# A hybrid decoder layer on one core: output-projection weights cast one step ahead, other casts and loads of the last two blocks put elsewhere

## The chip, the cores and the metric

The kernel runs on one core of one Trainium2 chip. Its time is the device time of one execution in microseconds (us), as the median of several runs. Beside the times stands one profiled execution, from which all rows below are taken. The engines are PE (matrix multiplications), DVE (VectorE), ACT (ScalarE), POOL (GpSimd) and SP, which here only issues transfers (DMA). Each engine works through its own list of instructions strictly in order: an instruction that waits holds back all that stand behind it on that engine.

## The reference

One layer of a decoder, for a prompt of 2048 tokens and 32 sample tokens (8 sequences of 4), all in float32. Cut to what the change touches:

```
z = rmsnorm(x, n1) @ w_in                 # split into hq, hf, hi, hg, sq, sk, sv, ga, gb
o_hg = hgrn_recurrence(q, log f, 1 - f, v, s0)      # 4 heads, state 128 x 128
y_a = (rmsnorm(o_hg) * silu(hg)) @ w_up_a           # 512 -> 1024
o_b = sliding-window attention with sinks (8 query heads, 2 kv heads)
y_b = o_b @ w_up_b                                   # 512 -> 1024
m = sigmoid(ga) * y_a + sigmoid(gb) * y_b
x = x + m @ w_o                                      # output projection, 1024 x 1024
x = x + relu(rmsnorm(x, n2) @ w_ff1)**2 @ w_ff2      # 1024 -> 4096 -> 1024
```

Of the sample tokens, each sequence starts from a state of its own and returns the new one.

## The kernel before

Activations lie transposed: features on the 128 partitions, tokens along the row. The prompt is worked in four blocks of 512 tokens (block 0 to 3; the last also carries the 32 sample tokens, so its row is 544 long and is worked in two segments of 288 and 256). After the four blocks the feed-forward part runs for all tokens. In blocks 2 and 3 (`zs` in the code) the gates ga and gb have been computed beforehand, between blocks 1 and 2, and are only loaded. In a tile's name the digit behind the letters is the block (`l_uab26`: block 2, unit 6); the profile leaves buffer numbers out, so there it is `l_uab`.

**Split precision.** Every matrix product is done as three: a float32 operand is split into a high part (ACT rounds it, line L257, tiles `h_...`) and a low part (DVE subtracts the high part from the original, L258, tiles `l_...`), and PE adds high*high, high*low and low*high. A weight unit of 128x1024 numbers is loaded by SP (`r_...`), and is usable by PE when ACT's cast and DVE's subtraction of it are done. `unit` and `unit_rows` issue the load, the cast and the subtraction. The three tiles of a unit take three of 12 buffers in one pool, so a load also waits until an older unit's last reader is done.

**Order.** The program is written in one order, and a scheduler puts each engine's instructions into a fixed list, by its own view of when they are ready. `pin(...)` (`keep_in_program_order`) keeps an instruction where the program has it. At run time nothing is reordered.

**One block**, in the order of time:

1. The input projections (`hi`, `hf`, `hg`, `sq`, `skv`) and the attention of four chunks (`b2c`: block 2), interleaved.
2. The levels of the recurrence (`hgrn_levels`): for m = 1, 2, 4, ... 64 PE does many small products (`lv_b2g0_1`, L771), and DVE two multiplications (L776, L777) and one predicated copy (L788) for each of two groups of heads. A level needs DVE's results of the one before. The sample tokens have two short levels of their own (`lv_b3s`).
3. The recurrence over four chunks: state update on DVE (L1204), normalisation (`on`, L1164), transposition (L1174). In block 3 the four heads of the sample tokens follow: PE multiplies the value products `vb` (made by DVE, L1226) with the keys (`us`, L1233), and DVE adds them to each state `S`. Between them stand matrix products of `y_b`.
4. `y_b` (`ybb`): eight column tiles j, with units of `w_up_b` (`ubb`) for two tiles each.
5. `y_a` (`yab`), called gate a here: eight column tiles, units of `w_up_a` (`uab`) for two tiles each. For each tile DVE gates (`ga`, L1258), POOL (for the last tiles DVE) adds the other branch (L1298), and `m` is split by ACT (L257) and DVE (L258).
6. The output projection (`wob`), in four steps n = 0, 2, 4, 6 of two column tiles, with two units each (`l_wob240` and `l_wob241` are the units of step 4). In step 0 the contraction index k runs outside, so both tiles end together; in the other steps the tiles follow each other. DVE evicts each tile and adds the residual row held in `x1` (L1394), ACT squares it for the next norm (L241 the first, L244 the others), POOL writes it out.

Beside this, blocks 0 and 2 prepare sums for the feed-forward part: `fr_load` loads rows, and `fr_sums` does four DVE additions (L605 to L608) whose results POOL writes out. `fr_at` says after which column tile they are written.

Of the kernel before, what the change touches and what calls it, by code (L numbers as in the profile page):

```python
# [16 lines left out]
P = 128  # L17
# [26 lines left out]
def tile_hybrid_step(  # L44
# [186 lines left out]
    class Norm:  # L231
# [6 lines left out]
        def add(u, x, eng=nc.gpsimd):  # L238
            if u.acc is None:
                u.acc = carry[:, 0:u.n]  # L240
                nc.scalar.activation(u.acc, x, AF.Square)  # L241
# [390 lines left out]
    for bi in range(nblk):  # L632
# [276 lines left out]
        fr_at = {("b", 0): lambda: fr_load(0), ("b", 5): fr_sums, ("b", 6): lambda: fr_load(1), ("a", 3): fr_sums} if zs and not odd else {}  # L909
# [229 lines left out]
        if smp:  # L1139
            gens.append(hgrn_levels(qS, kS, fS, aS, LEVELS[:2], NS, NS, f"{B}s", sres, SV[:, 2048:2144] if bt > gc else SV[:, 1024:1120]))  # L1140
        rnd, hg_at = 0, (2, 3, 4, 6)
        while gens:
# [12 lines left out]
            rnd += 1  # L1155

# [28 lines left out]
        for c in range(ncb):  # L1185
# [19 lines left out]
            on = hgrn_out(ops, P, N)  # L1205
            if tail is not None:
                hgrn_tail(*tail)
            tail = (on, P, fW, c * P, N)
        if smp:
# [8 lines left out]
            for h in range(HH):  # L1218
# [7 lines left out]
                nc.vector.tensor_tensor(  # L1226
                    vb[0:NS].rearrange("p (b e) -> p b e", b=DB),
                    vS[:, h * P:(h + 1) * P].unsqueeze(1).broadcast_to([NS, DB, P]),
                    m_b[0:NS].unsqueeze(2).broadcast_to([NS, DB, P]), ALU.mult)
# [149 lines left out]
        rings = [hg_ps, tp_ps if last_b else hg_ps, sw_ps, mm_ps, hg_ps, sw_ps, mm_ps, hg_ps]  # L1379
        for n in range(0, KD, 2):  # L1380
# [369 lines left out]
```

## Time and profile before

| what | us |
| --- | --- |
| median of 3 runs | 2822.58 (2820.04 to 2824.71) |
| span of the profiled execution, first to last instruction | 2810.0 |
| PE busy in it | 2730.1 |
| DVE busy | 1791.2 |
| ACT busy | 1110.0 |
| POOL busy | 490.9 |

The runs' times take in what lies before the first and behind the last instruction, so the median stands 12.6 us above the span of the profiled execution. In its trace block 1's output projection ends at about 740 us; block 2 lies at 965 to 1206, block 3 at 1206 to 1501, and the feed-forward part fills the rest.

### The profile page before, as it was taken

Reading aid. Unit: us, or ns where it says so; the run is one execution under the profiler, and the core shown is the slowest. Engines: PE = TensorE matmul, PEld = TensorE weight load, DVE = VectorE, ACT = ScalarE, POOL = GpSimd, SP = SyncE. Lnnn points to the kernel's source line nnn. Section 1 sums busy time; section 2 is a strip of 40 time slices with the busy share of each in tenths; the row PEclk is TensorE's granted clock in tenths of the full one; section 3 lists DMA queues with packets and bytes.
Section 4 is the critical chain, followed back from the end, with each engine's and each line's share of the span. In section 5 each row is a group of like instructions: output and inputs, shape, how many; then the busy total and the mean of one; then the engine's idle time right before and its main releaser. Section 6 shows DMA issues by size and latency. Waiting matters only on the chain.

```text
span 2810.0 us, 50089 instructions
## 1 busy us (share of the span) xinstructions
PE 2730.1 (97%) x20053; PEld 2403.9 (86%) x20053; DVE 1791.2 (64%) x2905; ACT 1110.0 (40%) x2070; POOL 490.9 (17%) x782
## 2 busy tenths in 40 slices
PE   8999999999999999899999999999999999999998
PEld 7778888788899977677898888878888999999998
DVE  5675746746774385637667777765567777654556
ACT  4542445423344353335334333434344233343332
POOL 1100211002300102320231221220012343320001
PEclk9999999999999999999999999999999999999999
DMA  5237662377743424652365544796566444485553
GB/s 190 75 103 237 208 198 76 97 242 256 251 126 115 144 76 149 219 160 67 105 210 184 181 145 150 265 317 222 190 200 215 147 161 135 155 291 184 189 187 119
DMA packets 344481, 487.60 MB, mean 174 GB/s; under 512 B 23432, under 2 KB 220824, under 8 KB 344248
## 3 DMA queue, kind: packets, MB, share of 16 engines
q1 hardware_dynamic: 289112, 329.10, 37.5%
q0 software_dynamic: 42880, 140.22, 13.8%
q10 hardware_dynamic: 12256, 15.08, 1.5%
q8 instruction: 157, 2.57, 0.4%
q14 instruction: 76, 0.62, 0.1%
HBM read 353.64 MB, written 130.68 MB: 172 GB/s over the span
## 4 chain that ended last, share of the span: by engine, by line
PE 78%; DMA 6%; DVE 6%; issue 5%; ACT 2%; POOL 2%; SPq 0%; POOLq 0%; DVEq 0%; ACTq 0%
PE f L1581 6%; PE f L1582 6%; PE f L1580 6%; PE fB_f L264 4%; PE fB_f L266 3%; PE fB_f L265 3%; PE fD_f L264 2%; PE fD_f L266 2%; PE fD_f L265 2%; PE ps_hfb L684 2%; PE fB_z L264 1%; PE fB_z L266 1%; PE fB_z L265 1%; PE wob L1390 1%; PE gab L166 1%
## 5 line engine op out<-in xcount | busy, mean ns | idle before, releaser
L1582 PE MATMUL f<-f2S,lw2T 128*128 128x264 f32 (+1 forms) x576 | 184.4, 320 | 2.0 <-DVE lw2T L152 2.0
L1580 PE MATMUL f<-f2S,hw2T 128*128 128x264 f32 (+1 forms) x576 | 184.5, 320 | 1.6 <-ACT hw2T L151 1.6
L1581 PE MATMUL f<-f2S,hw2T 128*128 128x264 f32 (+1 forms) x576 | 184.0, 319 | 0.0
L264 PE MATMUL fB_f<-S,w1T_f 128*128 128x264 f32 (+1 forms) x384 | 123.2, 322 | 3.1 <-ACT c_f L327 2.2
L152 DVE TENSOR_TENSOR lw2T<-lw2T,hw2T 128x1024 fp32r<-128x1024 f32 x64 | 78.2, 1224 | 69.7 <-ACT hw2T L151 68.8
L265 PE MATMUL fB_f<-S,w1T_f 128*128 128x264 f32 (+1 forms) x384 | 122.5, 319 | 0.0
L1580 PE MATMUL f<-f2A,h_w2B 128*128 128x264 f32 (+1 forms) x384 | 122.4, 319 | 0.0
L1581 PE MATMUL f<-f2A,h_w2B 128*128 128x264 f32 (+1 forms) x384 | 122.3, 319 | 0.0
L1582 PE MATMUL f<-f2A,l_w2B 128*128 128x264 f32 (+1 forms) x384 | 122.3, 318 | 0.0
L266 PE MATMUL fB_f<-S,w1T_f 128*128 128x264 f32 (+1 forms) x384 | 122.0, 320 | 0.0
L151 ACT CAST hw2T<-lw2T 128x1024 fp32r<-128x1024 f32 x64 | 67.2, 1051 | 137.2 <-DMA lw2T<-w_T 137.2
L1582 PEld LDWEIGHTS f<-f2S,lw2T 128*128 128x128 f32 x576 | 108.4, 188 | 10.4 <-DVE lw2T L152 2.9
L1580 PEld LDWEIGHTS f<-f2S,hw2T 128*128 128x128 f32 x576 | 108.8, 189 | 9.9 <-ACT hw2T L151 2.4
L1388 PE MATMUL wob<-m_b,h_wob 128*128 128x512 f32 (+2 forms) x320 | 113.1, 353 | 3.2 <-ACT h_wob L257 3.2
L1390 PE MATMUL wob<-m_b,l_wob 128*128 128x512 f32 (+2 forms) x320 | 112.4, 353 | 3.0 <-DVE l_wob L258 2.8
L1581 PEld LDWEIGHTS f<-f2S,hw2T 128*128 128x128 f32 x576 | 108.8, 189 | 7.6
L1389 PE MATMUL wob<-m_b,h_wob 128*128 128x512 f32 (+2 forms) x320 | 112.5, 352 | 0.0
L152 DVE TENSOR_TENSOR f2S<-f2S 128x1024 fp32r<-128x1024 f32 (+1 forms) x64 | 78.9, 1240 | 41.3 <-ACT f2S L151 40.9
L257 ACT CAST w1T_f<-w1r_f 128x512 fp32r<-128x512 f32 x128 | 77.1, 619 | 69.7 <-DVE w1r_f L300 29.7
L258 DVE TENSOR_TENSOR w1T_f<-w1r_f,w1T_f 128x512 fp32r<-128x512 f32 x128 | 87.4, 688 | 26.0 <-ACT w1T_f L257 25.7
L1507 POOL DMA_DIRECT2D u_A<-c_f x106 | 57.4, 541 | 236.1 <-DVE c_f L1491 225.1
L1507 POOL DMA_DIRECT2D u_S<-s_f x144 | 77.7, 541 | 109.0 <-DVE s_f L1502 92.4
(845 smaller groups left out, 9256.8 us busy)
## 6 DMA issues: line engine op xcount, KB each, us to landing
w1r_f<-w_ff SPq DMA_DIRECT2D x64, 512.0 KB
lw2T<-w_T SPq DMA_DIRECT2D x64, 512.0 KB
rw2B<-w_ff SPq DMA_DIRECT2D x48, 512.0 KB
f2S<-u_S SPq DMA_DIRECT2D x32, 528.0 KB
ws<-w_ff SPq DMA_DIRECT2D x32, 512.0 KB
r_wob<-w_o SPq DMA_DIRECT2D x32, 512.0 KB
f2S<-u_S SPq DMA_DIRECT2D x32, 512.0 KB
u_S<-s_f POOLq DMA_DIRECT2D x96, 132.0 KB, 2.3
```

The source lines that it names most:

```text
L152: pin(nc.vector.tensor_tensor(lo, F(lo), F(hi), ALU.subtract), on)
L258: pin(nc.vector.tensor_tensor(dl, src, F(dh), ALU.subtract), on)
L264: nc.tensor.matmul(ps, wh, ah, start=(first and k == 0), stop=False, skip_group_check=not first)
L265: nc.tensor.matmul(ps, wh, al, start=False, stop=False, skip_group_check=not first)
L266: nc.tensor.matmul(ps, wl, ah, start=False, stop=(last and k == 3), skip_group_check=not first)
L1388: nc.tensor.matmul(p, wh, ah, start=(k == 0), stop=False)
L1389: nc.tensor.matmul(p, wh, al, start=False, stop=False)
L1390: nc.tensor.matmul(p, wl, ah, start=False, stop=(k == KD - 1))
L1507: nc.gpsimd.dma_start(us[o][u.n // 4][u.n % 4 * P:(u.n % 4 + 1) * P, u.t0:u.t0 + u.ln], y_)
L1580: nc.tensor.matmul(ps, wh, ah, start=first, stop=False, skip_group_check=cont)
L1581: nc.tensor.matmul(ps, wh, al, start=False, stop=False, skip_group_check=cont)
L1582: nc.tensor.matmul(ps, wl, ah, start=False, stop=lastk, skip_group_check=cont)
```

## The change

1. The second `fr_sums` of block 2 is written after column tile 6 of gate a instead of tile 3.
2. In blocks 2 and 3 the units of `w_up_b` are issued at other places: unit 0 before the levels, unit 2 behind them, units 4 and 6 in chunks 1 and 2 of the recurrence. Units 2, 4 and 6 are pinned there.
3. The sample tokens' value products `vb` are pinned: they stay behind the recurrence.
4. In blocks 2 and 3 the residual rows `x1` are loaded during gate a (at j = 2, 4, 6, 6). Each load is held by a one-column DVE copy from a cast weight tile into `x1`, so that it can't be issued sooner. The loads are on POOL's queue, as before.
5. In all blocks the units of a step of the output projection are loaded and cast one step ahead, before the evictions of the step in front of it; the first eviction and the first square of a step are pinned behind them.

The diff, cut to its core:

```
-            ("b", 6): lambda: fr_load(1), ("a", 3): fr_sums} ...
+            ("b", 6): lambda: fr_load(1), ("a", 6): fr_sums} ...
...
+        def ub_unit(j, on=False):
+            return unit([... w_ub ... j * P:j * P + 256 ...], 4, f"ub{B}{j}", on)
+        ubs = {0: ub_unit(0)} if zs else {}
         rnd, hg_at = 0, (2, 3, 4, 6)
         while gens:                            # the levels
...
+        if zs:
+            ubs[2] = ub_unit(2, True)
...
             on = hgrn_out(ops, P, N)           # chunk c of the recurrence
+            if zs and c in (1, 2):
+                ubs[2 * c + 2] = ub_unit(2 * c + 2, True)
...
-                nc.vector.tensor_tensor(vb ...)
+                pin(nc.vector.tensor_tensor(vb ...))
...
-                ub = unit(... w_ub ...)
+                ub = ubs[j] if zs else ub_unit(j)
...
+                if j == 2:
+                    x1 = x1_tile()
+                for k in {2: (0,), 4: (2,), 6: (4, 6)}.get(j, ()):
+                    x1_load(k, F(ua[1])[:, 0, 0:1])   # copy into x1[:, k, 0:1], then the load of rows k, k+1
...
+        uo_next = wo_units(0)
         for n in range(0, KD, 2):
-            uo = [unit_rows(w_o, 4 * kh, 4, n * P, 2 * P, ...) for kh in range(2)]
+            uo = uo_next
...
+            ahead = n + 2 < KD
+            if ahead:
+                uo_next = wo_units(n + 2)
             for j in range(2):
-                    nc.vector.scalar_tensor_tensor(xo, ps[j][i], 0.5, xo, ALU.mult, ALU.add)
-                n2.add(x1[:, n + j], nc.vector if last_b else nc.gpsimd)
+                    pin(nc.vector.scalar_tensor_tensor(xo, ps[j][i], 0.5, xo, ...), ahead and i == j == 0)
+                n2.add(x1[:, n + j], nc.vector if last_b else nc.gpsimd, ahead and j == 0)
```

In the built program the change moves instructions on every engine. Three places on DVE matter below. A row is a line of the program, an operation, the tile written and the tiles read, and its size; the line numbers of the changed kernel are some 10 to 30 higher.

First, DVE in the levels of block 2, around m = 8 and 16. Before:

```order
L788 COPY_PREDICATED SV_b2_9399<-cu_88,lv_b2g1_8_10354 128x16x8
L779 TENSOR_TENSOR SV_b2_9399<-SV_b2_9399 128x32 x2
L975 TENSOR_TENSOR sg_11957<-snk_136,cf_86 128x8
L1146 COPY pb_b2_10047<-SV_b2_9399 128x1 x2
L977 TENSOR_REDUCE srows_11959<-sg_11957 128x2
L258 TENSOR_TENSOR l_ubb26_11016<-r_ubb26_11012,h_ubb26_11015 128x1024
L776 TENSOR_TENSOR W0_b2_9397<-W0_b2_9397,SV_b2_9399 128x4x8x16
L720 SCALAR_TENSOR_TENSOR W1_b2_9398<-tg_b2_2_0_p_10422,W1_b2_9398 128x512
```

The same place in the changed kernel:

```order
L779 TENSOR_TENSOR SV_b2_9399<-SV_b2_9399 128x64
L788 COPY_PREDICATED SV_b2_9399<-cu_88,lv_b2g1_8_10361 128x16x8
L779 TENSOR_TENSOR SV_b2_9399<-SV_b2_9399 128x32 x2
L1152 COPY pb_b2_10047<-SV_b2_9399 128x1 x2
L776 TENSOR_TENSOR W0_b2_9397<-W0_b2_9397,SV_b2_9399 128x4x8x16
L720 SCALAR_TENSOR_TENSOR W1_b2_9398<-tg_b2_2_0_p_10429,W1_b2_9398 128x512
L777 TENSOR_TENSOR W0_b2_9397<-W0_b2_9397,SV_b2_9399 128x4x8x16
L788 COPY_PREDICATED SV_b2_9399<-cu_88,lv_b2g0_16_10433 128x8x16
```

The cast of unit 6 of `w_up_b` no longer stands in the levels. The same holds for units 2 and 4, which stood at m = 1 and just ahead of m = 8, and for the three of block 3; of block 3's levels the first `vb` is gone as well. At m = 1 the order of the rest moved too: DVE's first two multiplications of that level now stand behind the last split of the attention (`ob`), and 59 of PE's 64 small products of that level behind the attention's last product, where before the 32 of the first group stood ahead of it.

Second, DVE in gate a of block 2, where unit 6 of `w_up_a` is cast. Before:

```order
L258 TENSOR_TENSOR m0_b2_11063<-ga_b2_10883,m0_b2_11063 128x512
L605 TENSOR_TENSOR fr12_11035<-fr11_11034 128x512
L1258 SCALAR_TENSOR_TENSOR ga_b2_10883<-ga_b2_10883,yab24_0_11165 128x512
L606 TENSOR_TENSOR fr12_11035<-fr12_11035,fr10_11033 128x512
L607 TENSOR_TENSOR fr11_11034<-fr10_11033,fr11_11034 128x512
L608 TENSOR_TENSOR fr10_11033<-fr10_11033,fr12_11035 128x512
L258 TENSOR_TENSOR l_uab26_11162<-r_uab26_11159,h_uab26_11161 128x1024
L258 TENSOR_TENSOR m1_b2_11064<-ga_b2_10883,m1_b2_11064 128x512
```

In the changed kernel:

```order
L1269 SCALAR_TENSOR_TENSOR ga_b2_10911<-ga_b2_10911,yab23_0_11137 128x512
L258 TENSOR_TENSOR m0_b2_11063<-ga_b2_10911,m0_b2_11063 128x512
L1269 SCALAR_TENSOR_TENSOR ga_b2_10911<-ga_b2_10911,yab24_0_11162 128x512
L258 TENSOR_TENSOR l_uab26_11157<-r_uab26_11154,h_uab26_11156 128x1024
L1297 COPY x1_b2_11117<-l_uab26_11157 128x1
L258 TENSOR_TENSOR m1_b2_11064<-ga_b2_10911,m1_b2_11064 128x512
```

The four `fr` additions have left the place ahead of `l_uab26`. From tile 0 on the gating of a tile and the split of the same tile alternate, where before tiles 0 and 1 were both gated ahead of the first split.

Third, DVE from the end of gate a to step 4 of the output projection in block 2. Before:

```order
L1258 SCALAR_TENSOR_TENSOR ga_b2_10883<-ga_b2_10883,yab27_0_11216 128x512
L1298 TENSOR_TENSOR ga_b2_10883<-ga_b2_10883,pb_b2_10047 128x512
L258 TENSOR_TENSOR m1_b2_11064<-ga_b2_10883,m1_b2_11064 128x512
L258 TENSOR_TENSOR l_wob201_11249<-r_wob201_11246,h_wob201_11248 128x1024
L1394 SCALAR_TENSOR_TENSOR x1_b2_11233<-wob20_0_11252,x1_b2_11233 128x512
L1394 SCALAR_TENSOR_TENSOR x1_b2_11233<-wob21_0_11253,x1_b2_11233 128x512
L258 TENSOR_TENSOR l_wob220_11322<-r_wob220_11319,h_wob220_11321 128x1024
L258 TENSOR_TENSOR l_wob221_11328<-r_wob221_11325,h_wob221_11327 128x1024
L1394 SCALAR_TENSOR_TENSOR x1_b2_11233<-wob22_0_11331,x1_b2_11233 128x512
L605 TENSOR_TENSOR fr22_11307<-fr21_11306 128x512
L258 TENSOR_TENSOR l_wob240_11411<-r_wob240_11408,h_wob240_11410 128x1024
```

In the changed kernel, in two pieces, with nothing between them:

```order
L258 TENSOR_TENSOR m1_b2_11064<-ga_b2_10911,m1_b2_11064 128x512
L605 TENSOR_TENSOR fr12_11035<-fr11_11034 128x512
L1319 TENSOR_TENSOR ga_b2_10911<-ga_b2_10911,pb_b2_10047 128x512
L606 TENSOR_TENSOR fr12_11035<-fr12_11035,fr10_11033 128x512
L607 TENSOR_TENSOR fr11_11034<-fr10_11033,fr11_11034 128x512
L608 TENSOR_TENSOR fr10_11033<-fr10_11033,fr12_11035 128x512
L258 TENSOR_TENSOR m1_b2_11064<-ga_b2_10911,m1_b2_11064 128x512
```

```order
L258 TENSOR_TENSOR l_wob201_11253<-r_wob201_11250,h_wob201_11252 128x1024
L258 TENSOR_TENSOR l_wob220_11309<-r_wob220_11306,h_wob220_11308 128x1024
L1423 SCALAR_TENSOR_TENSOR x1_b2_11117<-wob21_0_11257,x1_b2_11117 128x512
L258 TENSOR_TENSOR l_wob221_11315<-r_wob221_11312,h_wob221_11314 128x1024
L1423 SCALAR_TENSOR_TENSOR x1_b2_11117<-wob20_0_11256,x1_b2_11117 128x512
L1423 SCALAR_TENSOR_TENSOR x1_b2_11117<-wob23_0_11336,x1_b2_11117 128x512
L258 TENSOR_TENSOR l_wob240_11388<-r_wob240_11385,h_wob240_11387 128x1024
L258 TENSOR_TENSOR l_wob241_11394<-r_wob241_11391,h_wob241_11393 128x1024
L1423 SCALAR_TENSOR_TENSOR x1_b2_11117<-wob22_0_11335,x1_b2_11117 128x512
```

The `fr` additions now stand between the gating of the last tile and `l_wob201`. The first unit of step 2 is cast ahead of both evictions of step 0. Of the evictions of step 2 the one of the second tile (`wob23`), which is not pinned, stands ahead of both casts of step 4, and the pinned one of the first tile (`wob22`) behind them. On SP the loads of the third and fourth pair of output-projection units still follow the loads for the third `fr` sums, which wait until the results of the second have been written.

More of the change, by code (lines that the diff above doesn't have):

```diff
@@ L907, in fr_sums @@
             ff_sums(0, None, r, k, True, q)
-        fr_at = {("b", 0): lambda: fr_load(0), ("b", 5): fr_sums, ("b", 6): lambda: fr_load(1), ("a", 3): fr_sums} if zs and not odd else {}
+        fr_at = {("b", 0): lambda: fr_load(0), ("b", 5): fr_sums, ("b", 6): lambda: fr_load(1), ("a", 6): fr_sums} if zs and not odd else {}
         if not zs:
@@ L1140, in tile_hybrid_step @@
             gens.append(hgrn_levels(qS, kS, fS, aS, LEVELS[:2], NS, NS, f"{B}s", sres, SV[:, 2048:2144] if bt > gc else SV[:, 1024:1120]))
+        def ub_unit(j, on=False):
+            return unit(
+                [(kv * HD, (kv + 1) * HD, w_ub[kv * 256:(kv + 1) * 256, j * P:j * P + 256].rearrange("(k p) c -> p k c", p=HD)) for kv in range(NKV)],
+                4, f"ub{B}{j}", on)
+        ubs = {0: ub_unit(0)} if zs else {}
         rnd, hg_at = 0, (2, 3, 4, 6)
@@ L1282, in tile_hybrid_step, with x1_tile, x1_load @@
         a_acts = [(oa[:, 0, k, :], oa[:, 1, k, :]) for k in range(4)]
+        def x1_tile():
+            return op(6, F32, "x1_" + B)[:, 0:KD * T].rearrange("p (k t) -> p k t", k=KD)
+        def x1_load(k, after=None):
+            if after is not None:
+                nc.vector.tensor_copy(x1[:, k, 0:1], after)
+            nc.gpsimd.dma_start(x1[:, k:k + 2], kmaj(xT, k, 2, off[sb] + z0, T))
         mT = [op(2 + g, F32R, f"m{g}_{B}")[:, 0:8 * T].rearrange("p (s k t) -> p s k t", s=2, k=4) for g in range(2)]
@@ L1312, in tile_hybrid_step @@
         c0 = z0
-        x1 = op(6, F32, "x1_" + B)[:, 0:KD * T].rearrange("p (k t) -> p k t", k=KD)
-        for k in range(0, KD, 2):
-            nc.gpsimd.dma_start(x1[:, k:k + 2], kmaj(xT, k, 2, off[sb] + z0, T))
+        if not zs:
+            x1 = x1_tile()
+            for k in range(0, KD, 2):
+                x1_load(k)
         todo = []
@@ L1379, in tile_hybrid_step, with wo_units @@
         rings = [hg_ps, tp_ps if last_b else hg_ps, sw_ps, mm_ps, hg_ps, sw_ps, mm_ps, hg_ps]
+        def wo_units(n):
+            return [unit_rows(w_o, 4 * kh, 4, n * P, 2 * P, f"wo{B}{n}{kh}") for kh in range(2)]
+        uo_next = wo_units(0)
         for n in range(0, KD, 2):
-            uo = [unit_rows(w_o, 4 * kh, 4, n * P, 2 * P, f"wo{B}{n}{kh}") for kh in range(2)]
+            uo = uo_next
             ps = [[rings[j](f"wo{B}{j}_{t0}")[:, 0:ln] for (t0, ln) in segs] for j in (n, n + 1)]
@@ L1393, in tile_hybrid_step @@
                     xo = x1[:, n + j, t0:t0 + ln]
[L1394 to L1395 removed]
+                    pin(nc.vector.scalar_tensor_tensor(xo, ps[j][i], 0.5, xo, ALU.mult, ALU.add), ahead and i == j == 0)
+                n2.add(x1[:, n + j], nc.vector if last_b else nc.gpsimd, ahead and j == 0)
                 nc.gpsimd.dma_start(x1d[sb][(n + j) * P:(n + j + 1) * P, z0:z0 + T], x1[:, n + j])
```

13 lines of the change are left out of this document (5 added, 8 removed).

## The prediction

> **What bounds the kernel.** I began with the page: the span, the busy times, and the chain that ended last.
>
> ```profile
> span 2810.0 us, 50089 instructions
> PE 2730.1 (97%) x20053; PEld 2403.9 (86%) x20053; DVE 1791.2 (64%) x2905; ACT 1110.0 (40%) x2070; POOL 490.9 (17%) x782
> PE 78%; DMA 6%; DVE 6%; issue 5%; ACT 2%; POOL 2%; SPq 0%; POOLq 0%; DVEq 0%; ACTq 0%
> ```
>
> PE is busy for 2730.1 of 2810.0 us. The change adds no product and takes none away, so all it can win is in the 80 us in which PE stands still, and in stretches where PE runs at a lower clock. I therefore asked for PE's waits in the two places that the change rewrites most: blocks 2 and 3 (first fence), and block 1's output projection (second). The columns are: who waits, for whom, total us, times, longest.
>
> ```profile
> PE lv_b2g L771 <- DVE SV_b L788: 4.4, 1, 4.4
> PE yab L167 <- DVE l_uab L258: 3.8, 1, 3.8
> PE wob L1388 <- ACT h_wob L257: 3.2, 2, 1.7
> PE lv_b3s L771 <- issue: 2.4, 1, 2.4
> PE lv_b3g L771 <- issue: 2.1, 1, 2.1
> ...
> PE lv_b2g L771 <- issue: 1.3, 1, 1.3
> PE lv_b3g L771 <- DVE W_b L777: 1.1, 1, 1.1
> ...
> PE yab L165 <- ACT h_uab L257: 0.8, 1, 0.8
> ```
>
> ```profile
> PE wob L1390 <- DVE l_wob L258: 2.8, 2, 1.7
> ```
>
> Together 21.9 us: levels 11.3, gate a 4.6, output projections 6.0. Next I looked at the clock behind these waits, in a table by windows (window, length, PE busy, ..., granted clock, DMA share, GB/s).
>
> ```profile
> 1064.00:1067.50 3.50, 3.42 (x56) 2.55 (x58) 2.58 (x6) 3.38 (x9) 0.00 (x0) 0.52 0.02 5
> 1129.30:1134.20 4.90, 1.19 (x4) 0.65 (x4) 4.90 (x7) 0.62 (x1) 3.60 (x5) 0.79 0.34 131
> 1134.30:1141.10 6.80, 6.80 (x20) 5.45 (x21) 3.27 (x6) 1.80 (x3) 1.27 (x1) 0.65 0.85 256
> 1154.00:1158.00 4.00, 3.94 (x16) 2.96 (x17) 3.18 (x2) 2.34 (x3) 1.80 (x1) 1.00 0.28 104
> 1180.00:1183.40 3.40, 3.40 (x10) 2.64 (x9) 3.37 (x5) 2.51 (x3) 2.88 (x4) 0.50 0.21 79
> 1333.60:1340.40 6.80, 4.69 (x56) 4.25 (x46) 3.94 (x11) 1.63 (x3) 0.00 (x0) 0.50 0.02 5
> ```
>
> After four of the waits PE works at about half clock for 3.4 or 6.8 us. That loses 3.5 x 0.48 = 1.7 us in the levels of block 2, 6.8 x 0.35 = 2.4 in gate a while PE worked, 1.7 in the output projection, and up to 3.4 in the levels of block 3. After the 1.7 us wait at 1154 nothing was lost. So the upper bound of the change is 21.9 + 9.2 = 31 us. The Trainium skill (TensorE: Matmul & The Clock Gate, "What's actually happening") says that the clock falls to half after at least one idle window of about 3.4 us. The rows differ at 1180, where the wait ahead was under 2 us. By that rule the drops at 1180 and 1333 would not come from the short waits ahead of them and would stay, and the sum below would be 3.4 us smaller, -9.7.
>
> **Term 1, levels of block 2: -5.0.**
>
> ```profile
> 1054.49 0.16 DVE L977 TENSOR_REDUCE srows<-sg 128x2 f32<-128x8 f32 x1
> 1060.66 1.23 DVE L258 TENSOR_TENSOR l_ubb<-r_ubb,h_ubb 128x1024 fp32r<-128x1024 f32 x1 [6.01 <-ACT h_ubb L257]
> 1061.80 0.69 DVE L776 TENSOR_TENSOR W_b<-W_b,SV_b 128x512 f32<-128x512 f32 x1
> ```
>
> DVE stands 6.01 us in front of `l_ubb26`, because its load is late, and behind it wait the level's multiplications, for which PE then waits 4.4 us. The cast leaves this place: -4.4, and -1.7 of clock. Against that, the multiplications of m = 1 now start behind `ob` instead of ahead of it. That is about 1.2 us (two of 0.69, issued 0.6 apart) of DVE work that PE used to have ready; between 0 (fillers in PE's list cover it) and 2 us I take 1.1, since DVE's chain from there to m = 4 already left PE waiting 1.3 us.
>
> **Term 2, recurrence: +0.5.**
>
> ```profile
> 1080.17 1.12 DVE L1204 SCALAR_TENSOR_TENSOR state<-state,SV_b,u_b2o 128x128 f32<-128x128 f32 x4 [3.65 <-PE u_b2o L1199]
> ```
>
> The three casts of `w_up_b` now stand in its chunks, pinned, 1.23 us each, in front of the state updates. I take 0.5 in blocks 2 and 3 together: with the loads landed the casts fill gaps in which DVE waits for PE, such as the 3.65 us in front of the first state update. Ends: 0 and 3 x 1.23 = 3.7 per block. What happens if a load is late is a rival below.
>
> **Term 3, gate a of block 2 and step 0: -0.5.**
>
> ```profile
> 1114.96 0.69 DVE L1258 SCALAR_TENSOR_TENSOR ga_b<-ga_b,yab 128x512 f32<-128x512 f32 x1 [2.03 <-PE yab L167]
> 1117.68 0.69 DVE L1258 SCALAR_TENSOR_TENSOR ga_b<-ga_b,yab 128x512 f32<-128x512 f32 x1 [2.03 <-PE yab L167]
> ...
> 1129.53 0.68 DVE L1258 SCALAR_TENSOR_TENSOR ga_b<-ga_b,yab 128x512 f32<-128x512 f32 x1
> 1130.12 0.69 DVE L606 TENSOR_TENSOR fr<-fr,fr 128x512 f32<-128x512 f32 x1
> 1130.73 1.75 DVE L607 TENSOR_TENSOR fr<-fr,fr 128x512 f32<-128x512 f32 x1
> ...
> 1133.01 1.21 DVE L258 TENSOR_TENSOR l_uab<-r_uab,h_uab 128x1024 fp32r<-128x1024 f32 x1
> ```
>
> ```profile
> 1118.72 1.30 POOL L1298 TENSOR_TENSOR ga_b<-ga_b,pb_b 128x512 f32<-128x512 f32 x1
> 1122.08 2.20 POOL L1298 TENSOR_TENSOR ga_b<-ga_b,pb_b 128x512 f32<-128x512 f32 x1 [2.06 <-DVE ga_b L1258]
> ```
>
> ```profile
> 1127.66 0.62 ACT L257 CAST m_b<-ga_b 128x512 fp32r<-128x512 f32 x1 [2.72 <-POOL ga_b L1298]
> ```
>
> PE brings a tile each 2.72 us. In the new order DVE's gating and split of one tile alternate, so a tile takes 0.69 (gating) + 1.30 (POOL; 2.20 while DVE casts a unit) + 0.62 (ACT) + 0.69 = 3.3 to 4.2 us, and DVE falls behind PE. Walking down DVE's list from the row at 1114.96: tile 0 is split at 1118.3, tile 1 at 1121.6, `l_uab24` ends at 1123.5 (PE wants it at 1123.6), tile 2 is split at 1125.8, tile 3 at 1129.1, tile 4 gated at 1129.8, and `l_uab26` ends at about 1131, where it ended at 1134.2. PE wants it at 1129.1: a wait of 2.0 instead of 4.6. So PE enters step 0 at about 1136.
>
> ```profile
> 1141.14 0.39 PE L1388 MATMUL wob<-m_b,h_wob 128*128 128x512 f32 x1
> ```
>
> ```profile
> 1146.90 0.39 PE L1389 MATMUL wob<-m_b,h_wob 128*128 128x512 f32 x1
> 1147.13 0.39 PE L1390 MATMUL wob<-m_b,l_wob 128*128 128x512 f32 x1
> ```
>
> Before, PE entered step 0 at 1141.14, and first used `l_wob201` at 1147.13 without a wait. Now it wants it 6.0 us after 1136, at 1142. But from 1131 DVE has to wait for the sum of tile 4 (to 1132.6) and work off the split of tile 4, the gating of tile 5, `l_wob200`, the split of tile 5 (POOL's sum lands at 1136.3, ACT's cast at 1136.9), and then ten instructions started 0.61 apart (as 1129.53, 1130.12 and 1130.73 above): two gatings, two sums, two splits and the four `fr` additions. That is 1143.7, and `l_wob201` ends at 1144.9. So PE waits about 3 us in a new place. The time of that product moves from 1147.1 to 1144.9: -2.2, in which the old waits and the lost clock are all included. Such a wait is long enough to cost clock again: 0 (as after 1154) to 3.4; I take 1.7.
>
> **Term 4, steps 2 to 6 of block 2: -3.8.**
>
> ```profile
> 1152.36 0.63 ACT L241 ACTIVATE carry<-x_b 128x512 f32<-128x512 f32 x1 [6.86 <-DVE x_b L1394]
> 1152.90 1.03 ACT L257 CAST h_wob<-r_wob 128x1024 fp32r<-128x1024 f32 x1
> ...
> 1177.29 1.04 ACT L257 CAST h_wob<-r_wob 128x1024 fp32r<-128x1024 f32 x1 [2.76 <-DMA r_wob<-w_o]
> ```
>
> ACT's square stood ahead of step 2's first cast, and step 6's load came late; these are the two waits of 3.2 us in total. Both casts now stand ahead, and SP issues step 6's loads ahead of the rows of the last `fr` load: -3.2, and -1.7 of clock. But in step 4 the eviction of tile 3 stands ahead of `l_wob240`: it needs step 2 to be finished, then 0.69 + 1.2 us pass, while PE has four products that don't need it, 0.23 apart by the rows above: 1.9 - 0.9, with a little for the handing over +1.1.
>
> **Term 5, levels of block 3: -3.3.**
>
> ```profile
> 1327.62 1.21 DVE L1226 TENSOR_TENSOR vb<-vS,cf 32x1024 f32<-32x1024 f32 x1 [1.71 <-PE po_b3c L1108]
> ...
> 1332.64 1.20 DVE L258 TENSOR_TENSOR l_ubb<-r_ubb,h_ubb 128x1024 fp32r<-128x1024 f32 x1
> ```
>
> Here DVE never stands still for a load; it is simply full. Without `vb` the next split starts 0.5 us sooner (ACT's half of it is then the later one), and without `l_ubb` the following level starts 1.1 us sooner: -1.6 of the waits of 5.6. Of the 3.4 us of clock I take half, -1.7, between all and none.
>
> **Term 6, sample tokens: +1.0.** The first `vb` now stands between the last chunk and the first state, 1.21 us, where PE has little else to do: 0 to 1.2 us.
>
> **Term 7, block 1: -2.0** of the 2.8 us at its two `l_wob` waits, since the first cast now stands ahead of the eviction; the second still has an eviction in front of it. Block 0 shows no wait for these weights, block 3's output projection neither: 0, because step n's 128x512 products cover a cast there already. Between 0 and 2.8.
>
> **Residual rows and transfers: 0.** POOL issues four loads either way; before, they stood ahead of POOL's first two sums, now they stand between the sums, and the rows are needed only at the end of step 0. The seven added columns copied cost DVE about 0.1 us each and are in the rounding. They are covered as long as the load lands within the 20 us of gate a that remain.
>
> Sum: -5.0 + 0.5 - 0.5 - 3.8 - 3.3 + 1.0 - 2.0 = -13.1 us against the profiled execution's 2810.0, so a span of about 2797. What lies outside the span (12.6 us against the median of 2822.6) is not touched: 2809.5.
>
> **Rivals.**
>
> *No new waits* (the alternation in gate a is harmless because POOL's sums stay at 1.30, and the new wait for `l_wob201` doesn't appear). Then gate a gives all of its 4.6 + 2.4 instead of 0.5, step 4 costs nothing (-1.1), and block 3 loses no clock (-1.7): about -22, 2800. Against it: two POOL sums at 2.20 would have to vanish although the casts stay beside them.
>
> *Waits only change place.* The new wait for `l_wob201` grows when the `fr` additions run at 1.75, as one did at 1130.73 beside POOL (up to +4.3), brings 3.4 us of clock instead of 1.7, and the first level of block 2 costs 2 instead of 1.1: +6.9, hence about -6; with nothing won in block 3 (+3.3), -3: 2816 to 2820.
>
> *Slower: a late load inside the recurrence.* The wait of 6.01 us for `r_ubb` is not removed but goes with the cast into the recurrence, where DVE's state updates stand behind it and PE has only the few `y_b` products. This needs the load to land more than some 15 us later than it would by its place in SP's list, ahead of 1080 in block 2; the weight buffers that it needs come free when the `hgb` units are used up. If that happens in both blocks it costs 2 x (6 + 3.4) = 19, against -13: about +6, 2828. For it speaks that the load landed late once; against it, that the casts now come only in the gap ahead of 1080.17 and later, 16 us or more behind 1060.66.
>
> **Chances.** Forecast 0.55, no new waits 0.15, waits change place 0.20, late load 0.10. Changes within 0.2% (5.6 us) can't be told from none in this kernel. The forecast with its range (2803 to 2816) and the first rival count as faster, as does a quarter of the second: 0.75. The rest of the second is no change, 0.15, and the third is slower, 0.10. The range from 2799 to 2822 holds the forecast, most of the second rival and half of the first; the range of the forecast alone is 2803 to 2816.
>
> **What would show it.** In the new profile: no DVE wait before any `l_ubb`; the levels of block 2 at full clock at m = 8 to 16, with a wait at m = 1 or 2 of up to 2 us; `l_uab26` ended about 3 us sooner with a wait of 2; a PE wait on `l_wob` of about 3 us halfway through step 0; none at the start of steps 2 and 6, one of about 1 at step 4; block 3's levels with shorter but not vanished waits. The forecast is wrong if `yab` no longer waits at all, if the wait on `l_wob` is missing, or if DVE waits for ACT within the recurrence.

## The result, and the profile after

The changed kernel took 2824.91 us (median of 22 runs, 2819.62 to 2834.71), the kernel before, beside it on the same chip, 2821.41 (22 runs, 2813.08 to 2828.14). The ratio is 1.0019, with a 95% interval of 1.0011 to 1.0027: slower by about 5 us, within the 5.6 us that count as no change, where 13 us less were forecast. A second measurement (E1 below) gave 1.0036 [1.0021, 1.0051], 10 us.

The page of the changed kernel, the span, PE's line and the chain that ended last (its execution took 2833.14 us, one of the longest of this kernel):

```profile
span 2831.4 us, 50103 instructions
...
PE 2743.9 (97%) x20053; PEld 2413.4 (85%) x20053; DVE 1791.4 (63%) x2913; ACT 1108.6 (39%) x2070; POOL 488.9 (17%) x782
...
PE 77%; DVE 6%; DMA 6%; issue 5%; ACT 3%; POOL 2%; SPq 0%; POOLq 0%; DVEq 0%; ACTq 0%
```

PE's waits in the places on which the forecast spoke: block 2 from gate a to the end of the output projection and the turn to block 3 (first fence), and block 3's levels, recurrence and sample tokens (second). Columns as before.

```profile
PE ps_sqb_-1_11578 L191 <- ACT h_sqb L257: 2.2, 1, 2.2
PE wob L1416 <- DVE l_wob L258: 2.1, 2, 1.1
PE yab L167 <- DVE l_uab L258: 1.4, 2, 0.8
PE yab L165 <- ACT h_uab L257: 0.8, 1, 0.8
```

```profile
PE lx_b3g L805 <- issue: 1.9, 1, 1.9
PE lv_b3g L771 <- issue: 1.9, 1, 1.9
PE lv_b3s L771 <- issue: 1.8, 1, 1.8
PE o_smp L1235 <- DMA S<-state_hgrn: 1.6, 2, 1.5
PE lv_b3g L771 <- DVE W_b L777: 1.0, 1, 1.0
PE oT_smp L1181 <- DVE on_smp L1173: 0.6, 1, 0.6
```

The old waits of block 2 are gone or smaller: the 4.4 us at the levels and the 3.2 at `h_wob` are gone, the 3.8 at `l_uab` are 1.4 in two pieces. New are two of about 1 us on `l_wob`, and one of 2.2 behind the output projection, at the next block's first weights (`h_sqb`). In block 3 the waits without a shown releaser ("issue") became only a little shorter (1.8 and 1.9 instead of 2.4 and 2.1), `lx_b3g` is new among the long ones, and a load of a sample state came late.

The other loss lies where the forecast did not look. PE's waits after block 0's output projection, in the changed kernel:

```profile
PE ps_hib L191 <- DVE x_b L1423: 3.8, 2, 1.9
PE n_fb L216 <- POOL carry L245: 0.8, 1, 0.8
```

Here products of the next block's first projection (`ps_hib`) wait until DVE has evicted a tile (`x_b`) and so freed the buffer for products. I call the stretch from the last product of one block's output projection to the end of the next block's first projection a turn. From block 1 it ends at the first product of the gates computed ahead (`z`), from block 2 at the first product of block 3's projection `hi`.

To see where the time went, I took from each trace when PE starts the first and the last product of each stage. The table gives the length of each stage in a second profiled execution of the kernel before (column 2nd; its time 2819.24 us is close to the median), and the difference to it, in us, of the first and a third profile of before, of the changed kernel in two profiles (C1, C2), and of the experiments below. "Levels" holds the block's later projections and its attention too; "to FF" is all that lies ahead of the feed-forward part ("feed-fwd"), with block 0 (up to 2.3 us apart) and block 3's output projection (the same in all), which have no line of their own. Each column is one execution, and single executions of one kernel differ by some us:

```
stage        2nd   1st   3rd    C1    C2    E2    E3    E4    E5    E6    E7    E8   E11   E12   E13   E14
turn 0>1    25.5  -0.7  +0.4  +6.9  +4.7  +3.8  -0.5  +0.6  +3.6  -2.8  +5.8  +5.4  -1.3  -2.8  -2.8  -2.8
block 1    284.3  -0.6  -0.1  -0.9  -0.5  -1.1  +0.0  -0.7  -0.1  +0.2  -0.8  -0.4  -0.7  +0.0  +0.3  -0.0
wo 1        48.8  +0.0  +0.0  -3.4  -3.4  -3.4  +0.0  +0.0  +1.6  -2.1  -3.4  -3.4  -0.0  +1.1  +1.8  +3.8
turn 1>z    36.5  -0.0  -0.6  +5.8  +5.7  +3.9  -0.1  +0.1  +2.1  +3.9  +5.4  +3.6  -0.3  +0.2  -0.5  -0.1
z          203.2  +0.2  +0.5  +0.1  +1.4  +1.6  +0.6  +0.1  +1.3  +1.0  +0.5  +1.1  +0.4  +0.2  +0.5  +0.1
levels 2   113.4  -0.1  +1.0  -3.3  -4.8  +1.0  -4.1  -4.2  -3.9  -4.7  -4.4  -4.3  -4.1  -4.6  -4.6  -4.4
recur. 2    37.3  +0.0  +0.0  +0.5  +0.5  +0.0  +0.5  +0.6  +0.6  +0.5  +0.5  +0.5  +0.5  +0.5  +0.5  +0.5
gate a 2    29.1  +0.0  +0.5  -2.6  -2.6  -0.8  -2.6  -3.2  -4.2  -2.6  -2.6  -2.6  -1.6  -1.6  -0.4  -1.6
wo 2        50.3  -0.3  +0.5  -4.3  -4.3  -6.7  -4.3  -0.2  -1.1  -4.3  -4.3  -4.3  +0.2  -1.1  -6.9  -6.7
turn 2>3    45.9  +0.6  +0.3  +4.6  +5.3  +4.2  +3.8  +0.3  +7.1  +4.5  +5.3  +4.4  +0.2  -0.0  +4.1  +1.0
levels 3   130.4  -0.6  -0.3  +0.9  +0.4  +0.8  +2.3  +0.7  -1.3  +0.8  +1.6  +0.3  -0.2  +0.4  +0.6  +0.9
recur. 3    60.6  -1.8  -0.1  +5.1  +5.1  -1.8  +4.7  +3.0  +4.3  +7.2  +0.8  +4.1  -0.3  -1.6  -0.1  -1.5
gate a 3    24.2  +0.0  +0.0  +0.9  +0.9  +0.0  +0.9  +0.0  +0.9  +0.9  +1.6  +0.9  +0.0  +0.0  +0.0  +0.0
feed-fwd  1297.1  -2.8  -0.4  +4.2  +6.2  +3.7  +3.1  -0.6  +3.4  +1.4  +2.6  +3.1  +4.2  +0.9  +0.0  +8.1
to FF       1507  -4.6  +1.8  +9.7  +7.0  +0.1  -0.9  -4.6  +9.4  +1.0  +5.6  +4.8  -9.4  -9.4  -8.8 -11.4
```

In the changed kernel the stages that the forecast spoke of in blocks 1 and 2 gained 14 to 15 us (wo 1, levels 2, gate a 2, wo 2). The three turns lost 16 to 17, block 3 about 7.

### The profile page after: what moved, and what is told of

Same layout as the page of the kernel before. It is cut to its first block, busy times and chain, and to the rows that moved or that the text cites. A ratio compares the mean times of both kernels' runs of the same rounds, so it can differ in the third digit from the quotient of the medians.

```text
span 2831.4 us, 50103 instructions
## 1 busy us (share of the span) xinstructions
PE 2743.9 (97%) x20053; PEld 2413.4 (85%) x20053; DVE 1791.4 (63%) x2913; ACT 1108.6 (39%) x2070; POOL 488.9 (17%) x782
## 4 chain that ended last, share of the span: by engine, by line
PE 77%; DVE 6%; DMA 6%; issue 5%; ACT 3%; POOL 2%; SPq 0%; POOLq 0%; DVEq 0%; ACTq 0%
PE f L1611 6%; PE f L1610 6%; PE f L1609 6%; PE fB_f L264 4%; PE fB_f L266 4%; PE fB_f L265 4%; PE fD_f L264 2%; PE fD_f L266 2%; PE fD_f L265 2%; PE ps_hfb L684 2%; PE fB_z L264 1%; PE fB_z L266 1%; PE fB_z L265 1%; PE wob L1416 1%; PE gab L167 1%
## 5 line engine op out<-in xcount | busy, mean ns | idle before, releaser
L151 ACT CAST hw2T<-lw2T 128x1024 fp32r<-128x1024 f32 x64 | 67.2, 1051 | 137.2 <-DMA lw2T<-w_T 137.1
```

## The experiments

Two theories came from the first comparison. Theory A: the turns lose, because evictions and first casts of the next block stand behind moved casts and loads. Theory B: block 3 loses, to the moved casts and the pinned `vb`. Ratios are to the kernel before on the same chip, with 95% intervals.

**E1, the change again.** No edit.

> The changed kernel again, beside the kernel before on the same chip. Theory A (the loss lies at the turn from one block to the next: blocks 0 to 1 +7.6 us, 1 to z +5.8, 2 to 3 +4.0 in the first profile, because the eviction that frees the product buffers stands on DVE behind additions that wait for moved loads) and theory B (the loss lies in block 3, recurrence and sample tokens, +7.0): both stretches must come back within 1 us in a second profile, and the median is 3 to 8 us above before. Theory C (the profiled execution of the change was merely a long one): block turns and block 3 keep within 2 us of before in this profile, and the median is within 2 us of before. The +7 us of the feed-forward part, in which nothing is changed, should be gone (within 2 us) by A and B.

Measured: 2831.48 us, ratio 1.0036 [1.0021, 1.0051]. The turns lost 4.7, 5.7 and 5.3, block 3's recurrence 5.1 as in the first profile: A's and B's stretches came back, the first turn 2.2 us smaller than in the first profile. The feed-forward part stayed 6.2 above the second profile of before, which A and B had not expected, and the time lies above the 3 to 8 us that they allowed.

**E2, part 5 alone**, in all blocks, in the kernel before:

```
+        uo_next = wo_units(0)
         for n in range(0, KD, 2):
-            uo = [unit_rows(w_o, ...) for kh in range(2)]
+            uo = uo_next
...
+            ahead = n + 2 < KD
+            if ahead:
+                uo_next = wo_units(n + 2)     # then the evictions, the first of them pinned
```

> The kernel before with part 5 of the change alone (output-projection units one step ahead, in all blocks). Theory A: the turns from block 0 to 1, 1 to z and 2 to 3 lose 13 to 18 us together, the output projections themselves win 7 to 9, so the time is 5 to 9 us above before; block 3's recurrence is as before. Theory B: part 5 only wins; 5 to 9 us below before, and the turns are unchanged within 2 us.

Measured: 2825.75, ratio 1.0021 [1.0007, 1.0036]. The output projections gain 3.4 and 6.7 us, the turns lose 3.8, 3.9 and 4.2. In block 0, where part 5 wins nothing, it only loses; in block 1 it gives all of its win back, in block 2 about two thirds. Block 3's recurrence is not longer. This is theory A for part 5 in its place, not in its size: the turns lost 11.9 us where 13 to 18 were expected, and up to the feed-forward part this profile is level with before (+0.1).

**E3, part 5 in blocks 2 and 3 only**, the rest as changed: `uo_next = wo_units(0) if zs else None`.

> The changed kernel with the units of the output projection one step ahead in blocks 2 and 3 only; blocks 0 and 1 as before. Theory A: the turns 0 to 1 and 1 to z come back to before (-13 us), and the win of 3.5 us in block 1's output projection is lost: 7 to 11 us below the changed kernel, so 2 to 6 below before. Theory B: the time is that of the changed kernel or 2 to 4 us above it.

Measured: 2821.14, ratio 1.0004 [0.9991, 1.0017]. The first two turns are those of before (-0.5, -0.1), the third still loses 3.8, block 3's recurrence 4.7. As A expected for the turns; the time is that of before, where 2 to 6 us less were expected.

**E4, part 2 alone** (the units of `w_up_b`) in the kernel before: `ubs = {0: ub_unit(0)} if zs else {}` and so on, nothing else.

> The kernel before with part 2 alone (units of w_up_b issued at other places in blocks 2 and 3). Theory B with the casts as cause: levels of block 2 -3 us, recurrence and sample tokens of block 3 +4 to +7: 1 to 5 us above before. Theory A, or B with the pinned vb as cause: levels -3, recurrence +0.5 to +1 a block, so 1 to 3 us below before.

Measured: 2822.29, ratio 1.0002 [0.9989, 1.0016]. Levels of block 2 -4.2, and gate a -3.2, which I had put down to the moved `fr` additions; block 3's recurrence +3.0 without any pin on `vb`, between the +4 to +7 and the +0.5 to +1 that the two theories gave. On balance part 2 gains in block 2 and loses in block 3. The time shows neither: the profiled execution is the shortest of the 12 (2814.64 us).

**E5, the last step not ahead.** In the changed kernel the units of step 6 are issued at their old place: `ahead = n + 4 < KD`. DVE's list at the end of block 0 is then that of before, row by row.

> The changed kernel, but the units of the last step (6) of each output projection are issued at their old place; those of steps 2 and 4 stay one step ahead. Theory A, sharpened: the early cast of step 6's units is what lets the next block's casts move up by one in DVE's list, in front of the evictions. Then the turns 0 to 1 and 1 to z come back to within 1 us of before (-5 and -5 us against the changed kernel's profile), block 1's output projection keeps its win of 3.5, and the time is 7 to 12 us below the changed kernel's. Rival (the turns are lost to the steps in front as well, or to the lookahead's transfers): the turns keep more than half of their loss, and the time is less than 4 us below.

Measured: 2823.47, ratio 1.0011 [1.0000, 1.0023]. The sharpened theory fell in this profile: with before's own list on DVE the turn 0 to 1 still lost 3.6 us, and block 1's output projection lost its win (+1.6). So the order on DVE alone does not explain this turn. But this profile is of the longest of E5's 11 executions (2832.16 us), and another could show less.

**E6, row loads held.** What DVE's evictions stand behind at the end of block 0 is seen in the changed kernel's DVE rows (start, length, ..., idle time before and its releaser):

```profile
360.69 1.23 DVE L258 TENSOR_TENSOR l_hib<-r_hib,h_hib 128x1024 fp32r<-128x1024 f32 x1 [2.93 <-ACT h_hib L257]
361.83 0.68 DVE L1423 SCALAR_TENSOR_TENSOR x_b<-wob,x_b 128x512 f32<-128x512 f32 x1
...
367.26 0.71 DVE L543 TENSOR_TENSOR na_z<-na_z,nx_z 128x528 f32<-128x528 f32 x1 [1.27 <-ACT nx_z L539]
367.88 0.68 DVE L1423 SCALAR_TENSOR_TENSOR x_b<-wob,x_b 128x512 f32<-128x512 f32 x1
...
373.76 0.71 DVE L543 TENSOR_TENSOR na_z<-na_z,nx_z 128x528 f32<-128x528 f32 x1 [1.31 <-ACT nx_z L539]
374.38 0.68 DVE L1423 SCALAR_TENSOR_TENSOR x_b<-wob,x_b 128x512 f32<-128x512 f32 x1
```

The sums of squares for blocks 2 and 3 (`na_z`) are written into block 1, but the scheduler draws them into the end of block 0. Each waits for a loaded row, its row buffer (there are two) is loaded anew only when the addition is done, and the weight loads of the next block stand on SP between these row loads. In the second profile of before the same three evictions start at 357.82, 363.93 and 370.45, 3.9 to 4.0 us sooner. The edit holds the first row load of each of the two sums until block 1's first `y_b` tile:

```
+            elif k == 0 and u.hold is not None:
+                nc.vector.tensor_copy(u.x[:, 0:1], u.hold)      # u.hold = pb[:, 0, 0:1] of block 1
             nc.sync.dma_start(u.x, xT[...])
```

> The changed kernel, but the loads of rows for the norm sums of blocks 2 and 3 (L534) are held until block 1's first y_b tile by a one-column copy, so that no such addition (L543) stands at the end of block 0. If these additions with their loads make the evictions late there, the turn 0 to 1 comes back to before within 1 us (-5 us), while the turn 1 to z stays; what the sums cost in block 1, between 0 and 3 us, is seen there. If the early casts of the next block alone make them late, the turn keeps 3 us or more of its loss of 5.

Measured: 2822.93, ratio 1.0014 [1.0004, 1.0023]. The turn is 2.8 us shorter than before's, 7.5 to 9.7 shorter than the changed kernel's; the turn 1 to z kept 3.9. The sums, now in block 1, cost it about 1 us and its output projection 1.3. The same window at this turn (window, length, PE busy, ..., granted clock, DMA share, GB/s) in the second profile of before, in E5, in the changed kernel and in E6:

```profile
366.00:382.00 16.00, 13.69 (x62) 10.75 (x61) 10.80 (x13) 7.77 (x11) 4.08 (x4) 1.00 0.86 262
```

```profile
366.00:382.00 16.00, 12.70 (x46) 9.58 (x45) 10.30 (x13) 7.63 (x11) 3.68 (x4) 0.79 0.82 251
```

```profile
366.00:382.00 16.00, 11.41 (x32) 8.09 (x31) 10.98 (x13) 8.29 (x12) 4.34 (x5) 0.69 0.79 242
```

```profile
366.00:382.00 16.00, 16.00 (x77) 13.26 (x76) 5.73 (x6) 4.23 (x5) 3.26 (x3) 1.00 0.38 114
```

PE has no wait left at this turn, so the chain of row loads makes it, in the kernel before too. By E2 and E3 part 5 is what lengthens it. E5's turn shows how small a delay suffices. The waits for the eviction there, in the second profile of before and in E5:

```profile
PE ps_hib L191 <- DVE x_b L1394: 1.2, 1, 1.2
```

```profile
PE ps_hib L191 <- DVE x_b L1422: 2.2, 1, 2.2
```

With one microsecond more of waiting the clock was 0.79 instead of 1.00 over these 16 us. On the 12.7 us in which PE worked that is 12.7 x 0.21 = 2.7 us, with the wait 3.7, against a turn that is 3.6 longer. The chain itself was not late in E5: its last eviction of block 0 starts at 370.01 instead of 370.45, but block 0's last product came 1.4 us sooner. In the first profile of before that product came as early, and the chain was early too; why it was not in E5 is open.

**E7, part 2 in block 2 only**, the rest as changed: `zu = zs and not smp` in place of `zs` at the four places of `ub_unit`.

> The changed kernel with the units of w_up_b moved in block 2 only; in block 3 they stay where they were before, vb is still pinned. If the three casts cost block 3's recurrence and sample tokens their 7 us, that stretch comes back to within 2.5 us of before and the time is 3 to 6 us below the changed kernel's. If the pinned vb costs most of it, the stretch keeps more than 4 us of its loss, and the time is within 3 us of the changed kernel's.

Measured: 2832.16, ratio 1.0039 [1.0026, 1.0053]. Block 3's recurrence came back (+0.8 against the second profile), so part 2 in block 3 cost most of what was lost there. Up to the feed-forward part this profile is 1.4 to 4.1 us below the changed kernel's, but the time is not: the expected 3 to 6 us were missed, and only 5 runs were timed.

**E8, no pin on `vb`**, the rest as changed.

> The changed kernel without the pin on vb. If vb costs little beside the casts (the run with part 2 alone lost 4.9 us in that stretch without the pin, the changed kernel 7.0), block 3 from the first recurrence product to gate a gains about 2 us, at the price of up to 1 in its levels, and the time is 0 to 2 us below the changed kernel's. If the pin is the main cause, it gains 4 us or more.

Measured: 2826.26, ratio 1.0021 [1.0009, 1.0033]. Recurrence +4.1 instead of +5.1: by this one profile the pin costs about 1 us, part 2 (E4, E8) 3 to 4.

**E9 and E10, the kernel before, profiled again.** No edit, one execution each.

> The kernel before, profiled again. All profiles so far, with the feed-forward part unchanged in each, show it 2 to 9 us longer than the first profile of before. If that profile was an untypically short execution, this one shows the feed-forward part longer by 2 to 6 us, and a wait for the eviction at the turn 0 to 1 of 1 to 3 us instead of 0.9. If the changes lengthen the feed-forward part, it agrees with the first profile within 1.5 us.

> The kernel before, profiled a third time, to see how far two executions of one kernel differ stage by stage: by the theory of an untypically short first profile, the feed-forward part is again 2 to 6 us longer than in it, and blocks 2 and 3 agree within 1.5 us.

Measured: 2819.24 and 2820.66 us, spans 2817.4 and 2818.9. The first profile of before was the untypical one: 7.4 us shorter than the second, of which 2.8 in the feed-forward part, 1.8 in block 3's recurrence, 0.7 at the first turn. The span lies only 1.8 us below the time of the same execution, so most of the 12.6 us between the first profile's span and the median is not time outside the span.

**E11, part 2 in block 2 alone**, in the kernel before, and **E12, the same with E6's held row loads.**

> The kernel before with part 2 in block 2 alone; block 3, the output projections, vb and the residual rows as before. By the stage table of the run with part 2 alone: levels of block 2 -4.1, its recurrence +0.5, gate a -3.2, block 3 unchanged (-1 to +1): 5 to 7 us below before. If the loads of the casts hit the next stage instead, it stays within 2 us of before.

> The same with the row loads of the norm sums held until block 1's first y_b tile. If their chain makes the evictions late at the end of block 0 in the kernel before too, the turn 0 to 1 gains 2 to 4 us more: 7 to 11 us below before. If the chain cost only beside the changed output projection, the time is that of the run without the hold, or up to 3 us above it, for the sums then stand in block 1's gates.

Measured: E11 2817.90, ratio 0.9986 [0.9976, 0.9996]; E12 2814.93, ratio 0.9977 [0.9966, 0.9989]. By the medians E11 gains 4.6 us where 5 to 7 were expected: its levels gained 4.1, but gate a 1.6, not 3.2. E12 gains 7.6, at the low end of the 7 to 11 expected; its turn 0 to 1 is 2.8 shorter, E11's 1.3.

**E13, E12 with part 5 in block 2 alone**, and **E14, the same with the loads of the third and fourth `fr` sums on POOL's queue:**

```
-            pin(nc.sync.dma_start(x, h2d[b][...]))
+            pin((nc.gpsimd if k >= 2 else nc.sync).dma_start(x, h2d[b][...]))
```

> The kernel of the last run (part 2 in block 2, held row loads) with part 5 in block 2 alone. By the stage tables, block 2's output projection gains 4 us and the turn 2 to 3 gives 3 to 5 back, at a wait of 2 to 3 us for the first cast of the next block (h_sqb) that was not there before: the time stays within 2 us of that run without part 5. If the loss at that turn came from blocks 0 and 1's changed timing instead, the 4 us stay won.

> The same, but the loads of the third and fourth fr sums are issued by POOL instead of SP; in the built order the next block's first weight load then stands ahead of them, and its cast on ACT moves from behind the second splitting of the next block's activations (L151) to ahead of it. If the load's place behind the fr loads is what gives the gain back at the turn 2 to 3, the wait for h_sqb after the last product of the output projection vanishes and 2 to 4 us more stay won. If the splits (L151) and their own loads end last anyway, another wait of the same length takes its place. POOL's sums for the norm may come later by the wait of its queue: 0 to 2 us.

Measured: E13 2812.06, ratio 0.9963 [0.9948, 0.9979]; E14 2813.04, ratio 0.9963 [0.9950, 0.9977]. In E13 the output projection of block 2 gains 6.9 us and the turn 2 to 3 gives 4.1 back, with nothing edited in blocks 0, 1 and 3. What PE waits for after the last product, in E13 and in E14:

```profile
PE ps_sqb_-1_11576 L191 <- ACT h_sqb L257: 2.5, 1, 2.5
```

```profile
PE ps_sqb_-1_11576 L192 <- DVE l_sqb L258: 1.7, 1, 1.7
```

ACT's rows at the end of the output projection, in the second profile of before, in E13 and in E14 (L151 splits the next block's activations):

```profile
1184.63 1.03 ACT L257 CAST h_sqb<-r_sqb 128x1024 fp32r<-128x1024 f32 x1
...
1192.53 1.09 ACT L151 CAST hT_b<-hT_b 128x1088 fp32r<-128x1088 f32 x1
```

```profile
1181.33 1.08 ACT L151 CAST hT_b<-hT_b 128x1088 fp32r<-128x1088 f32 x1
1182.32 1.04 ACT L257 CAST h_sqb<-r_sqb 128x1024 fp32r<-128x1024 f32 x1
```

```profile
1174.31 1.03 ACT L257 CAST h_sqb<-r_sqb 128x1024 fp32r<-128x1024 f32 x1
...
1183.99 1.08 ACT L151 CAST hT_b<-hT_b 128x1088 fp32r<-128x1088 f32 x1
1184.98 1.04 ACT L257 CAST h_sqb<-r_sqb 128x1024 fp32r<-128x1024 f32 x1
```

The weights of block 3's first projection are loaded behind the `fr` loads in before too, but there the first cast stands ahead of the split of activations; with part 5 it stands behind it, and behind the square (L244) of a late tile. With the `fr` loads off SP, that cast runs 8 us sooner, ahead of the split, and the turn costs 1.0 instead of 4.1. So three quarters of the loss hang on the place of this load and of its cast, which moved together in E14: which of the two counts was not separated. The median of E14 is nevertheless that of E13. E14's profile is of the longest of its 8 executions (2815.90 us) and has 8.1 us more in the feed-forward part and 2.0 more in block 1's output projection than E13's. Whether its other executions share that is not known. E12, E13 and E14 are all faster than the kernel before, by 7 to 10 us; between E13 and E14 the runs show no difference.

## Why the prediction was wrong

**The base.** "What lies outside the span (12.6 us ...) is not touched" was the first error. 1.8 us lie outside; the rest was that the profiled execution was a short one (E9, E10). It moves the base of the forecast and not its -13 us, but it means that the waits were read in a short execution.

**Term 1 (levels of block 2, -5.0):** right, -3.3 and -4.8. The wait of 4.4 is gone, and PE runs at a clock of 1.00 from 1046 to 1082. Three "issue" waits at `lv_b2g` are left: 1.1 us at m = 2, as the price of 1.1 for the late start was forecast, 0.3 at m = 4, where 1.3 stood, and 0.9 at m = 32.

**Terms 3 and 4 (-0.5 and -3.8, together -4.3):** gate a -2.6 and the output projection -4.3, together -6.9 (term 3 reaches into the output projection, so the two can't be matched one by one). The place was right, the size too cautious. `l_wob201` did make PE wait in a new place, but 1.1 us instead of 3; step 4's wait is there (1.0 against 1.1 forecast), none at steps 2 and 6. The clock that was reckoned as lost again was not lost: in the window of the output projection, in the second profile of before and in the changed kernel,

```profile
1143.70:1194.00 50.30, 46.47 (x193) 36.55 (x192) 29.04 (x31) 15.92 (x20) 17.73 (x22) 0.97 0.66 228
```

```profile
1146.20:1192.10 45.90, 43.84 (x192) 35.69 (x191) 30.11 (x35) 13.65 (x17) 16.48 (x23) 1.00 0.76 256
```

By the rule of the Trainium skill quoted in the prediction (TensorE: Matmul & The Clock Gate, "What's actually happening") the drop behind the short wait at step 6 would have stayed without it; it went with the wait, so the row decides. E4 and E11 show 3.2 and 1.6 us of gain in gate a with part 2 and without the moved `fr` additions, so the walk down DVE's list named the wrong part of the change for some of it. No run has part 1 alone.

**Term 5 (levels of block 3, -3.3):** wrong in sign, +0.9 and +0.4, by its clock. The waits came as forecast, 1.7 us less, where 1.6 were taken; but PE was busy 2.6 us longer. Windows from block 3's first `hi` product to the recurrence, second profile of before, then changed:

```profile
1239.90:1370.30 130.40, 121.36 (x1654) 104.05 (x1652) 82.68 (x197) 58.81 (x180) 13.01 (x17) 0.97 0.33 95
```

```profile
1242.70:1374.00 131.30, 123.97 (x1654) 106.24 (x1651) 78.35 (x193) 55.42 (x177) 10.32 (x17) 0.95 0.30 85
```

The stretch at half clock behind the waits without a shown releaser grew from about 7 us (1336 to 1343) to about 10 (1338 to 1348), where half of it was forecast as won back; why is open. These waits of 2.4 and 2.1 were put down to DVE being full. Taking 2.4 us of DVE work out left them at 1.8 and 1.9, so that was not the whole of it; what the one at `lv_b3g` goes with stands in the last section.

**Terms 2 and 6 (recurrence and sample tokens):** block 2 lost 0.5, which had been forecast for both blocks together. Block 3 +5.1, against half of that 0.5 and the 1.0 of term 6. The pin on `vb` cost about 1 (E8), as term 6 said. A step that failed is term 2's "the casts fill gaps": in block 3, part 2 cost 3 to 4 us (E4, E7, E8). PE was busy longer at a lower clock as well as idle longer; windows from the first recurrence product to gate a, second profile of before, then changed:

```profile
1370.30:1430.90 60.60, 59.13 (x488) 51.26 (x479) 35.82 (x73) 14.85 (x57) 9.12 (x14) 0.97 0.42 123
```

```profile
1374.00:1439.70 65.70, 61.52 (x485) 52.32 (x478) 40.27 (x77) 17.63 (x60) 9.11 (x14) 0.95 0.43 130
```

Idle 4.2 instead of 1.5; the rest is busy time, 2.4 us. None of PE's waits there is for a cast: `lx` waits 1.9 instead of 0.8, the loads of sample states 1.6 instead of 0.6, and `oT_smp` 0.6. The wait at `lx` comes with part 2 in block 3: it is 0.8 where block 3 has its old order (E7, E11) and 1.9 to 2.4 in the changed kernel, E3, E4 and E8. Of the rivals the "late load inside the recurrence" named the place, and its sign came: DVE waited there for ACT's casts of `w_up_b`. But that was 1.9 us in two pieces over blocks 2 and 3, not 6 us in each, and block 2 lost only 0.5.

**Residual rows (0):** gate a of block 3 lost 0.9 to 1.6 us in every profile with part 4 and nothing in those without it; part 4 was not run alone.

**Term 7 (block 1 -2.0, block 0 nothing):** wo 1 gained 3.4, more than forecast. But the sum ended at the last product of each output projection. "Block 0 shows no wait for these weights ...: 0" priced what PE waits for inside the stage, and not what the moved casts and loads push back: the evictions that free the next stage's buffers, and the next block's first weights. That is the step that failed: 15.7 to 17.3 us at three turns, more than all gains in blocks 1 and 2, and no rival had it. Part 5 is shown to be the cause at all three (E2, where it alone cost 11.9; E3 for the first two, E13 for the third). For the turns 0 to 1 and 2 to 3, E6 and E14 also show through what: the chain of row loads, and the place of the next block's first load and cast. For the turn 1 to z what part 5 works through is not shown. The rows of the changed kernel show the like there, an eviction behind a cast that waits for its load:

```profile
728.42 1.57 DVE L258 TENSOR_TENSOR l_sqb<-r_sqb,h_sqb 128x1024 fp32r<-128x1024 f32 x1 [1.07 <-ACT h_sqb L257]
...
731.76 0.68 DVE L1423 SCALAR_TENSOR_TENSOR x_b<-wob,x_b 128x512 f32<-128x512 f32 x1
```

No run isolates that.

**Open:** the feed-forward part, whose code is the same in all, took 1294 to 1305 us in the profiles (rows with "feed-fwd"), with waits for the `w_ff2` weights and for evictions that differ from one execution to the next. Whether the changed kernel's 4 to 6 us there are chance is not settled.

## What to carry to other kernels

A cast or load that is moved ahead is paid for by whatever it is moved past: follow each queue it passes, SP's included, over the end of the stage, down to the evictions that free the next stage's product buffers and the next stage's first weights. Look for a chain of small loads through few buffers near that end (row, square, addition, next row); it runs at its own pace, and whatever stands between its links does too. And take two or three profiled executions of one kernel before a difference of under 1% is put down to a stage.

## What the runs showed of the hardware

At the turn 0 to 1 the granted clock over the 16 us from 366 to 382 went with the longest wait for the eviction. In the ten profiles in which that was 1.6 us or less, or none (before three times, E3, E4, E6, E11 to E14), it was 1.00; in the six with 1.9 us or more (the changed kernel twice, E2, E5, E7, E8) it was 0.69 to 0.89. E5 with 2.2 us has a turn 3.0 us longer than E4 with 1.6. The length alone does not decide, and no threshold follows: at step 6 of block 2's output projection PE worked at 0.50 for 3.4 us behind a wait of 1.5 (first profile of before), while waits of 1.7 at step 2 (the same profile) and at the turn from 1 to z (changed) were followed by 1.00.

Most of PE's waits without a shown releaser go with the loading of the program. The trace has loads of 16384 bytes on the queue for instructions. In eight profiles (before three times, the changed kernel twice, E4, E6, E7), 26 of the 34 such waits of 0.7 us or more in and just behind the levels of blocks 2 and 3 end 1.2 to 1.6 us after one of these loads has landed, those at `lv_b2g`, `lv_b3g`, `lx_b3g` and `ps_hgb`; the new wait at `lx_b3g` ends 1.3 us after one that landed at 1375.78:

```profile
1377.07 0.58 PE L805 MATMUL lx_b3g<-W_b 128*32 128x1 f32 x49 [1.93 <-issue]
```

The eight at `lv_b3s` do not fit. So moving instructions also shifts where such a load falls among the small products. This is read from the times alone; no run isolates it.
